# Seven products instead of eight for V and P as well: a fused decoder layer on one Trainium2 core

## The chip, the cores and the metric

The kernel runs on one core of one Trainium2 chip. The metric is the device time of one execution in microseconds (us). Three runs of the kernel before the change gave a median of 1529.9 us (1529.4 to 1530.04). All work is done by that core's engines: PE (matrix products), DVE (elementwise work on vectors), ACT (activations, copies and casts), POOL (a few small operations), and SP, whose queue issues most of the transfers.

## The reference

One decoder layer on a sequence of 256 tokens with 2048 features, in float32. What matters here is the input projection, whose columns are cut into K, Q, V, Z, P and two gates, and what becomes of them:

```python
h = rmsnorm(x, norm_mix_w[l])
proj = jnp.einsum('bsd,de->bse', h, w_in[l])
q, k, v, z, b_raw, a_raw, p_in, g_a, g_b = jnp.split(proj, splits, axis=-1)
qkv = jax.nn.silu(causal_dwconv(jnp.concatenate([q, k, v], axis=-1), conv_qkv_w[l]))
...
o = gated_delta_rule(q, k, v, g_log, beta).astype(x.dtype)
o = rmsnorm(o, gdn_norm_w[l]) * jax.nn.silu(z.reshape(bsz, seq, N_HEADS, HEAD_DIM))
pooled = causal_multiscale_pool(p_in.reshape(bsz, seq, N_POOL_GROUPS, POOL_GROUP_DIM))
y_b = jnp.einsum('bsgc,gcd->bsgd', pooled, pool_w[l]).reshape(bsz, seq, D_POOL) * pool_scale[l]
mixed = jax.nn.sigmoid(g_a) * y_a + jax.nn.sigmoid(g_b) * y_b
x = x + jnp.einsum('bsd,de->bse', mixed, w_out[l])
```

Behind it come a gated feed-forward part with 5632 inner features and a last norm.

## The kernel before, in words

**Groups, blocks, tiles.** The heads are worked on in four groups of four (`g` 0 to 3 in the code, group one to four here). A group has seven blocks of 512 columns of `w_in`, in the order K, Q, V, P, GB (gate b), Z, GA (gate a), and a small pool product. A block's weights come as eight *tiles* of 256 input features x 512 columns (512 KB each, `raw`, four buffers). ACT casts each to a rounded high part (`whi`, line 343) and DVE subtracts to get the low part (`wlo`, line 354, the *split*); both have three buffers. PE then does 12 matmuls of 128x128 by 128x512 for a plain tile: two halves of the features, two halves of the tokens, and three passes (high by high, high by low of x, low by high of x), in `gemm_a`.

**The pair of K and Q.** In groups two to four, K and Q already share a cheaper form. Two tiles of K and the same two of Q (features 0 to 511) are a 2x2 by 2x2 block product: eight block products of six matmuls each, 48, if done plainly. `pair_product` does seven products of six matmuls instead, called T1, 11, T2, 21, T3, 22 and T4. Their weights are either one of the four tiles as it is (11, 21, 22) or a difference of tiles that DVE makes (`up_sum`, line 270): T1 to T4. The four tiles are loaded into buffers of other things that are free then (`quad`, homes `KQ_HOMES`: `crow`, `mv`, `pu`, `pa`). Between the products come a copy of the first result (`own`, ACT), a copy into the second block's bank, a sum `u` (DVE, line 429), a copy of `u` into the other block's bank (ACT, line 418) before product 21 begins, and one more sum (DVE, line 431). The seven products stand in three parts: `KQ_FIRST` between the last tiles of the GA of the group before, `KQ_MIDDLE` (21, T3, 22) while GA's banks are being read out, and `KQ_THEN` (tile 2, T4, tiles 3 to 7) as the rest of K. Q then has its tiles 2 to 7.

**What goes on beside it.** `later` is a list of closures that `gemm_a` runs at a given tile (`flush`): a block's read-out is followed by its convolution (`conv_silu`: eight PE transposes, four ACT and twelve DVE instructions `cy`, a tanh, a DVE product), V's shifted copies through memory (`v_moved`, `v_conv`, tiles `mv`), and `mixed`, which turns the finished output `sz` of the group before on PE and splits it into `mhi`/`mlo`. The delta rule of a group (`gdn`) is a generator that `gemm_a` steps twice per tile; it begins with a load of `crow` and eight ACT exponentials (`dec`, line 958) and ends in the next group with `so`, `ro`, eight ACT scalings of `vt` (line 1340) and two DVE products on `sz`.

**What sets the order.** Every engine works strictly in the order of its own list. In the part in question a scheduler writes these lists from the dependencies and its own estimates when the program is built; `tc.issue_after` adds an order by hand.

## Time and profile before

| | |
|---|---|
| median of three runs | 1529.9 us |
| the profiled execution, its own time | 1531.07 us |
| its span, first to last instruction | 1529.3 us |
| PE busy | 1517.6 us, 99% of the span |
| DVE busy | 1263.2 us, 83% |
| ACT busy | 884.6 us, 58% |
| POOL busy | 73.0 us, 5% |
| moved by DMA | 313.60 MB, 205 GB/s on the mean |
| groups two to four run from about | 176 us to 700 us |

In the profile's rows a number behind a name such as L354 is the line of the kernel, a row of groups reads "line engine operation out<-in shapes xcount | busy us, mean ns of one | idle time of the engine ahead of it and what ended that", and a row of the timeline reads "start us, duration us, engine, line, ...". Matmuls overlap each other, so their recorded 390 ns or so are not what one of them costs; the distance of their starts is.

### The profile page before, as it was taken

The page shows a single profiled execution, that of the slowest core. Times are in us where ns is not written, and L with a number is a line of the kernel's source. Part 1 is how long each engine was busy: PE and PEld are TensorE (multiplying, and loading weights), DVE is VectorE, ACT ScalarE, POOL GpSimd, SP SyncE. Part 2 cuts the span into 40 slices and gives each one's busy share as a digit, 9 for nine tenths or more (in the row PEclk, how much of TensorE's full clock was granted, in tenths as well). Part 3 has the DMA queues.
Part 4 walks back from the last instruction along what each step waited for, and adds up shares of the span by engine and source line. Part 5 has one row for each costly group of instructions (what it writes and reads, how often), then busy time and mean ns, then how long its engine had stood idle before and what let it go on. Part 6 is the DMA issues. An engine that isn't in the chain of part 4 may idle for free.

```text
span 1529.3 us, 20251 instructions
## 1 busy us (share of the span) xinstructions
PE 1517.6 (99%) x7272; PEld 1252.7 (82%) x7272; DVE 1263.2 (83%) x1775; ACT 884.6 (58%) x1145; POOL 73.0 (5%) x97
## 2 busy tenths in 40 slices
PE   9999999999999999999999999999999999999998
PEld 8878888888878878788888888888888888888876
DVE  6779868888588877877567999999998886989896
ACT  7556556455556456454455677667666665555553
POOL 1000000100100001000000000000000011010200
PEclk9999999999999999999999999999999999999999
DMA  8777648784667746776588646666457468566762
GB/s 276 207 231 223 196 142 232 223 256 127 194 211 215 235 134 201 220 199 187 171 258 311 192 166 220 220 211 216 152 164 235 143 215 274 174 224 210 239 199 99
DMA packets 170097, 313.60 MB, mean 205 GB/s; under 512 B 23650, under 2 KB 27010, under 8 KB 169870
## 3 DMA queue, kind: packets, MB, share of 16 engines
q1 hardware_dynamic: 160864, 283.17, 58.7%
q0 software_dynamic: 7344, 27.27, 5.6%
q10 hardware_dynamic: 1790, 1.89, 0.4%
q8 instruction: 57, 0.93, 0.2%
q14 instruction: 42, 0.34, 0.1%
HBM read 303.33 MB, written 8.95 MB: 204 GB/s over the span
## 4 chain that ended last, share of the span: by engine, by line
PE 94%; issue 2%; DVE 2%; DMA 1%; ACT 1%; POOL 0%; POOLq 0%; DVEq 0%; ACTq 0%
PE psg L439 27%; PE psm L404 14%; PE psm L402 13%; PE psm L403 13%; PE psm L1523 7%; PE psg L1523 7%; PE psm L439 3%; PE psm L582 1%; PE psm L1591 1%; PE psg L481 1%; DVE wlo L354 1%; PE psg L969 1%; PE psg L971 0%; DMA vrow<-ev 0%; ACT whi L343 0%
## 5 line engine op out<-in xcount | busy, mean ns | idle before, releaser
L343 ACT CAST whi<-raw 128x1024 fp32r<-128x1024 f32 x408 | 427.7, 1051 | 346.2 <-PE psm L403 192.6
L354 DVE TENSOR_TENSOR wlo<-raw,whi 128x1024 fp32r<-128x1024 f32 x406 | 494.8, 1222 | 134.8 <-ACT whi L343 126.2
L343 ACT CAST whi<-quad 128x1024 fp32r<-128x1024 f32 x203 | 213.0, 1052 | 159.0 <-PE psg L439 45.4
L354 DVE TENSOR_TENSOR wlo<-quad,whi 128x1024 fp32r<-128x1024 f32 x203 | 246.8, 1223 | 39.8 <-ACT whi L343 36.6
L402 PE MATMUL psm<-whi,xhl 128*128 128x512 f32 x384 | 150.3, 392 | 0.1
L403 PE MATMUL psm<-whi,xhl 128*128 128x512 f32 x384 | 150.2, 391 | 0.0
L404 PE MATMUL psm<-wlo,xhl 128*128 128x512 f32 x384 | 139.9, 393 | 0.5 <-DVE wlo L354 0.4
L439 PE MATMUL psg<-whi,fhl 128*128 128x512 f32 x504 | 127.1, 389 | 0.0
L439 PEld LDWEIGHTS psg<-whi,fhl 128*128 128x128 f32 x504 | 94.6, 188 | 19.7
L270 DVE TENSOR_TENSOR quad<-quad,quad 128x1024 f32<-128x1024 f32 x84 | 102.5, 1220 | 0.1
L402 PEld LDWEIGHTS psm<-whi,xhl 128*128 128x128 f32 x384 | 72.1, 188 | 15.6 <-ACT whi L343 0.5
L404 PEld LDWEIGHTS psm<-wlo,xhl 128*128 128x128 f32 x384 | 71.7, 188 | 15.9 <-DVE wlo L354 1.3
L403 PEld LDWEIGHTS psm<-whi,xhl 128*128 128x128 f32 x384 | 72.1, 188 | 15.3 <-issue 0.5
L439 PE MATMUL psg<-wlo,fhl 128*128 128x512 f32 x252 | 69.8, 389 | 0.0
L439 PE MATMUL psg<-whi,ups 128*128 128x512 f32 x216 | 58.1, 391 | 0.2 <-DVE psg L1544 0.2
L439 PEld LDWEIGHTS psg<-wlo,fhl 128*128 128x128 f32 x252 | 47.3, 188 | 9.9
L1523 PE MATMUL psm<-whi,hhi 128*128 128x512 f32 (+1 forms) x140 | 54.2, 387 | 0.0
L1523 PE MATMUL psm<-whi,hlo 128*128 128x512 f32 (+1 forms) x140 | 53.7, 386 | 0.0
L402 PE MATMUL psm<-whi,mhi 128*128 128x512 f32 x128 | 50.6, 397 | 0.0
L1523 PE MATMUL psm<-wlo,hhi 128*128 128x512 f32 (+1 forms) x140 | 50.2, 386 | 0.0
L403 PE MATMUL psm<-whi,mlo 128*128 128x512 f32 x128 | 50.0, 390 | 0.0
L404 PE MATMUL psm<-wlo,mhi 128*128 128x512 f32 x128 | 48.3, 392 | 0.0
(455 smaller groups left out, 2983.3 us busy)
## 6 DMA issues: line engine op xcount, KB each, us to landing
raw<-in_w_in_dram SPq DMA_DIRECT2D x212, 512.0 KB, 4.4
raw<-in_w_up_dram SPq DMA_DIRECT2D x104, 512.0 KB, 4.9
quad<-in_w_up_dram SPq DMA_DIRECT2D x72, 512.0 KB, 5.0
raw<-in_w_down_dram SPq DMA_DIRECT2D x56, 512.0 KB, 4.7
raw<-in_w_out_dram SPq DMA_DIRECT2D x32, 512.0 KB, 4.8
quad<-in_w_down_dram POOLq DMA_DIRECT2D x32, 512.0 KB, 5.4
mv<-vrow SPq DMA_DIRECT2D x12, 512.0 KB, 4.8
quad<-in_w_in_dram SPq DMA_DIRECT2D x12, 512.0 KB, 7.4
```

The costliest lines, as they stand in the source:

```text
L270: nc.vector.tensor_tensor(out_, plus_, minus_, op=ALU.subtract)
L343: last_cast[0] = nc.scalar.copy(hi, raw).ins
L354: last_split[0] = nc.vector.tensor_tensor(lo, raw, hi.bitcast(F32), op=ALU.subtract).ins
L402: mm(ps[:, t, :], lh(k, t), hi[:, kk, :], start=(k == 0), stop=False, **seeded)
L403: mm(ps[:, t, :], ll(k, t), hi[:, kk, :], start=False, stop=False, **seeded)
L404: mm(ps[:, t, :], lh(k, t), lo[:, kk, :], start=False, stop=(k == nk - 1), **seeded)
L439: mm(ps, lhs(kk), w[n][:, kk], start=(first and n == 0 and kk == 0 and lhs is high), stop=False, skip_group_check=True)
L481: nc.tensor.transpose(pt[:, ff, t * P : (t + 1) * P], src[:, t, f * P : (f + 1) * P], ident)
L582: mm(ps_k0[:, t, :], part(k, t), w[:, kk, :], start=(k == 0 and w is hi and part is xh), stop=(k == KD - 1 and w is lo))
L969: mm(pg0, kq[:, h, 0, 0:P], kq[:, h, :, :], start=True, stop=True)
L1523: mm(ps[:, cs], lhs(kk), part_[:, kk, cs], start=(first and kk == 0 and n == 0), stop=(last and kk == 1 and n == 2), skip_group_check=shared)
L1591: nc.tensor.transpose(out_[f // 2][:, f % 2, t * P : (t + 1) * P], e[:, t, f * P : (f + 1) * P], ident)
```

## The change

V and P of groups two to four become a pair like K and Q. V's T1, 11 and T2 go between Q's last three tiles, 21, T3 and 22 stand while Q is read out, and V's own block becomes tile 2, T4 and tiles 3 to 7; P keeps tiles 2 to 7. The four tiles of this pair are loaded into `mv`, `pu`, `pa` and `dec0`, and its sum `u` into `crow`. Since V's block is now run with a flush at tile 3 (it was tile 1), as is P's, the closures behind them start two tiles later, and the generator gets no steps in the products. `mixed` of the group before is kept back in `mixing` and run behind K's convolution instead of ahead of it. The first product on `sz` behind GA is tied behind the split issued last.

```diff
+    up_w = {(pair, g): [cols(w_in[0], base + 512 * g, KD) for base in bases]
+            for pair, bases in (("kq", (C_K, C_Q)), ("vp", (C_V, C_P))) for g in range(1, 4)}
...
-            if g and base == C_K:
-                srcs += [("up", ("kq", g), step, 0) if isinstance(step, str) else tiles[step]
+            if g and base in (C_K, C_V):
+                pair = "kq" if base == C_K else "vp"
+                srcs += [("up", (pair, g), step, 0) if isinstance(step, str) else tiles[step]
                          for step in KQ_MIDDLE + KQ_THEN]
+            elif g and base == C_Q:
+                srcs += tiles[2:5]
+                srcs += [("up", ("vp", g), step, 0) if isinstance(step, str) else tiles[step] for step in KQ_FIRST]
             else:
-                srcs += tiles[2:] if g and base == C_Q else tiles
+                srcs += tiles[2:] if g and base == C_P else tiles
...
-    KQ_HOMES = ("crow", "mv", "pu", "pa")
+    KQ_HOMES = {"kq": ("crow", "mv", "pu", "pa"), "vp": ("mv", "pu", "pa", "dec0")}
...
-            bank["u"] = mp.tile([P, 512], F32, tag="dec0", name=nm("u"))
+            bank["u"] = mp.tile([P, 512], F32, tag=bank["u_home"], name=nm("u"))
...
-                ps = gemm_a(xh, xl, KD, range(2, 8), pair_bank["ps"][1], 3)
+                ps = gemm_a(xh, xl, KD, range(2, 5), pair_bank["ps"][1], 3)
+                pair_bank.update(ps=(pm(), None), u_home="crow")
+                kq_steps(KQ_FIRST, ps)
             e = evict(ps)
             convs.append(conv_silu(e, kind, g, dst))
             if g:
                 later.append(lambda conv=convs[-1]: sum(1 for _ in conv))
+                later.extend(mixing)
+                mixing.clear()
...
+        if g:
+            pair_bank["ps"] = pair_bank["ps"][0], pm()
+            kq_steps(KQ_MIDDLE, None)
...
-        e = evict(gemm_a(xh, xl, KD), rsh)
+        if g:
+            ps = pair_bank["ps"][0]
+            kq_steps(KQ_THEN, ps)
+        else:
+            ps = gemm_a(xh, xl, KD)
+        e = evict(ps, rsh)
...
-        ps = gemm_a(xh, xl, KD)
+        ps = gemm_a(xh, xl, KD, range(2, 8), pair_bank["ps"][1], 3) if g else gemm_a(xh, xl, KD)
...
-        nc.vector.scalar_tensor_tensor(sz, ta, 1.0, sz, op0=ALU.add, op1=ALU.mult)
+        with tc.issue_after(last_split[0]):
+            nc.vector.scalar_tensor_tensor(sz, ta, 1.0, sz, op0=ALU.add, op1=ALU.mult)
...
         if g < 3:
-            later.append(mixed)
+            mixing.append(mixed)
```

How the lists move is shown at three places, all in group three, around the end of Q and the start of V. In these rows `wlo<-raw` is the split of a plain tile, `wlo<-quad` that of a product's weights, `quad<-quad` a difference of tiles, `cy` a step of a convolution.

DVE before, in the first half of V: the splits of V's plain tiles, and the steps of K's convolution among them.

```order
L354 TENSOR_TENSOR wlo_3976<-raw_3972,whi_3974 128x1024
L910 SCALAR_TENSOR_TENSOR cy_3771<-psg_3761,cqw,cy_3771 128x255
L910 SCALAR_TENSOR_TENSOR cy_3771<-psg_3766,cqw,cy_3771 128x255
L910 SCALAR_TENSOR_TENSOR cy_3771<-psg_3761,cqw,cy_3771 128x254
L354 TENSOR_TENSOR wlo_4005<-raw_4001,whi_4003 128x1024
L910 SCALAR_TENSOR_TENSOR cy_3771<-psg_3766,cqw,cy_3771 128x254
```

DVE now, from V's sum `u` to the splits of V's tile 2 (`wlo_3963`) and T4 (`wlo_3974`). In this stretch the splits of T3 (`wlo_3928`) and 22 (`wlo_3951`), a difference, both small sums of the pair, `ro` of the group before and K's convolution follow one another.

```order
L435 TENSOR_TENSOR u_3924<-psm_3853,own_3864 128x512
L916 SCALAR_TENSOR_TENSOR cy_3783<-psg_3773,cqw,cy_3783 128x253
L360 TENSOR_TENSOR wlo_3928<-quad_3679,whi_3926 128x1024
L276 TENSOR_TENSOR quad_3659<-quad_3719,quad_3659 128x1024
L1162 TENSOR_TENSOR ro_3313<-ro_3313,so_3499 128x8
L916 SCALAR_TENSOR_TENSOR cy_3783<-psg_3778,cqw,cy_3783 128x253
L360 TENSOR_TENSOR wlo_3951<-quad_3699,whi_3949 128x1024
L916 SCALAR_TENSOR_TENSOR cy_3783<-psg_3773,cqw,cy_3783 128x255
L437 TENSOR_TENSOR psm_3947<-psm_3853,own_3864 128x512
L360 TENSOR_TENSOR wlo_3963<-raw_3959,whi_3961 128x1024
L360 TENSOR_TENSOR wlo_3974<-quad_3659,whi_3972 128x1024
L1165 TENSOR_SCALAR ro_3313<-ro_3313,rsq 128x4 x2
```

K's convolution has come forward into the stretch of the seven products, and more DVE work stands between one split and the next than before.

SP before, in group three: `crow` is issued without a wait of its own, among the loads of weights.

```order
L243 DMA raw_3893<-in_w_in_dram 128x2x512 [waits DMAHW6_49,DVE_49]
L243 DMA raw_3941<-in_w_in_dram 128x2x512 [waits DMAHW7_49,DVE_49]
L945 DMA crow_3961<-crd 128x1024
L862 DMA taps_3888<-in_conv_qkv_w_dram 128x512 [waits DVE_49]
L862 DMA taps_3888<-in_conv_qkv_w_dram 128x512
L243 DMA raw_3972<-in_w_in_dram 128x2x512 [waits DMAHW0_49,DVE_49]
```

SP now: the load of `crow` waits for ACT, for the copy that reads `u`, which lies in the same buffer. The next weights stand behind it.

```order
L249 DMA raw_4007<-in_w_in_dram 128x2x512 [waits DMAHW6_49,DMAHW2_49,DVE_49]
L249 DMA raw_4049<-in_w_in_dram 128x2x512 [waits DMAHW3_49,DVE_49]
L951 DMA crow_4069<-crd 128x1024 [waits Activation_49]
L249 DMA raw_4080<-in_w_in_dram 128x2x512 [waits DMAHW4_49,DVE_49]
L249 DMA raw_4109<-in_w_in_dram 128x2x512 [waits DMAHW5_49,DVE_49]
L249 DMA raw_4141<-in_w_in_dram 128x2x512 [waits DMAHW6_49,DVE_49]
```

ACT before, in group three: the scalings of `vt` come first, then four casts, and then the exponentials `dec`, of which two of eight are shown.

```order
L1340 ACTIVATE vt_2322<-psg_3379,ro_3206 128x128 x4
L1340 ACTIVATE vt_2322<-vt_2322,ro_3206 128x128 x4
L343 CAST whi_3829<-raw_3827 128x1024
L343 CAST whi_3847<-raw_3845 128x1024
L343 CAST whi_3865<-raw_3863 128x1024
L343 CAST whi_3895<-raw_3893 128x1024
L958 ACTIVATE dec_704_3959<-crow_3961,ncum 128x128
L958 ACTIVATE dec_705_3960<-crow_3961,ncum 128x128
```

ACT now, from the copy of `u` on: the casts of V's tile 2, T4 and tile 3, then the `dec` rows, of which the first two are shown.

```order
L424 COPY psm_3946<-u_3924 128x512
L913 ACTIVATE cy_3783<-psg_3773,cqw 128x256
L349 CAST whi_3961<-raw_3959 128x1024
L349 CAST whi_3972<-quad_3659 128x1024
L913 ACTIVATE cy_3783<-psg_3778,cqw 128x256
L349 CAST whi_3991<-raw_3989 128x1024
L964 ACTIVATE dec_734_4067<-crow_4069,ncum 128x128
L964 ACTIVATE dec_735_4068<-crow_4069,ncum 128x128
```

Behind the last of the eight `dec` rows come the scalings of `vt`, and only then the cast of V's tile 4 (`whi_4009`).

```order
L964 ACTIVATE dec_735_4068<-crow_4069,ncum 128x128
L1360 ACTIVATE vt_2403<-psg_3482,ro_3313 128x128 x4
L1360 ACTIVATE vt_2403<-vt_2403,ro_3313 128x128 x4
L349 CAST whi_4009<-raw_4007 128x1024
L349 CAST whi_4051<-raw_4049 128x1024
```

So `dec`, which used to stand five rows behind `vt`, now stands ahead of it, six rows behind the copy of `u` on which its load depends. Group four's lists read the same here; in group two the `vt` rows are long done.

More of the change, by code (lines that the diff above doesn't have):

```diff
@@ L85 @@
     KQ_THEN = (2, "T4", 3, 4, 5, 6, 7)
-    up_w = {("kq", g): [cols(w_in[0], base + 512 * g, KD) for base in (C_K, C_Q)] for g in range(1, 4)}
+    up_w = {(pair, g): [cols(w_in[0], base + 512 * g, KD) for base in bases]
+            for pair, bases in (("kq", (C_K, C_Q)), ("vp", (C_V, C_P))) for g in range(1, 4)}
     srcs = []
@@ L158 @@
     quads_behind = {}
-    for g in range(1, 4):
-        sums_behind[first_part(("kq", g)) - 1] = [(("kq", g), "T1", 0)]
-        for i in range(4):
-            quads_behind[first_part(("kq", g)) - 6 + i] = [(("kq", g), i)]
+    for pair in up_w:
+        if isinstance(pair, tuple):
+            sums_behind[first_part(pair) - 1] = [(pair, "T1", 0)]
+            for i in range(4):
+                quads_behind[first_part(pair) - 6 + i] = [(pair, i)]
     for n, src in enumerate(srcs):
@@ L257, in quad_load @@
         if isinstance(c, tuple):
-            home = mp.tile([P, 2, 512], F32, tag=KQ_HOMES[i], name=nm("quad"))
+            home = mp.tile([P, 2, 512], F32, tag=KQ_HOMES[c[0]][i], name=nm("quad"))
         else:
@@ L1189 @@
     pair_bank = {}
+    mixing = []
     def kq_steps(steps, ps, flush=3):
@@ L1316 @@
             ps = gemm_a(xh, xl, KD, range(5))
-            pair_bank["ps"] = pm(), None
+            pair_bank.update(ps=(pm(), None), u_home="dec0")
             kq_steps(KQ_FIRST, ps, 1)
```

## The prediction

> **What bounds the kernel now.** I read the page's totals first, then the chain that ended last, then the timeline around the longest waits.
>
> ```profile
> span 1529.3 us, 20251 instructions
> ...
> PE 1517.6 (99%) x7272; PEld 1252.7 (82%) x7272; DVE 1263.2 (83%) x1775; ACT 884.6 (58%) x1145; POOL 73.0 (5%) x97
> ...
> PEclk9999999999999999999999999999999999999999
> ```
>
> PE is the bound at a full granted clock, so time is won by fewer matmuls and lost by anything PE has to wait for. The chain of waits, merged, prices a matmul:
>
> ```profile
> 239.33 1.75 PE psg L481 x16
> ...
> 527.64 1.36 PE psm L439 x6
> ...
> 545.53 1.23 DVE sz L1323
> ...
> 546.76 1.15 DVE wlo L354
> ...
> 1315.35 2.72 PE psm L1523 x12
> ```
>
> Six matmuls take 1.36 us and twelve 2.72, 0.227 each; a transpose 0.109. Two of these rows are DVE's: there PE waited. In the timeline that is the longest wait of the groups:
>
> ```profile
> 547.95 0.50 PE L404 MATMUL psm<-wlo,xhl1a 128*128 128x512 f32 x1 [1.41 <-DVE wlo L354]
> ```
>
> It lies in the pair of K and Q ahead of group four: a product on `sz` (1.23) stood ahead of a split. So the same form of pair already costs PE some waiting where DVE has other work. How much room DVE has where the new pair goes, at the end of Q and the start of V:
>
> ```profile
> core 0: us, PE busy (x) PEld busy (x) DVE busy (x) ACT busy (x) POOL busy (x), PEclk, DMA share, GB/s
> 205.00:245.00 40.00, 40.00 (x207) 34.04 (x206) 23.15 (x31) 24.36 (x44) 2.86 (x3) 1.00 0.69 203
> 380.00:420.00 40.00, 40.00 (x206) 34.02 (x205) 21.53 (x29) 23.01 (x43) 4.42 (x3) 1.00 0.66 203
> 556.00:596.00 40.00, 40.00 (x216) 33.86 (x215) 21.80 (x28) 22.06 (x39) 4.56 (x3) 1.00 0.62 183
> ```
>
> On the mean DVE is idle for 17 to 18 of 40 us here. What counts is how far it runs ahead of PE, the *lead*: from the end of a split to PE's first use of it.
>
> ```profile
> 327.55 1.23 DVE L354 TENSOR_TENSOR wlo<-raw,whi 128x1024 fp32r<-128x1024 f32 x1 [0.29 <-ACT whi L343]
> ...
> 332.84 0.61 PE L404 MATMUL psm<-wlo,phi 128*128 128x512 f32 x2
> ...
> 554.79 3.50 DVE L354 TENSOR_TENSOR wlo<-raw,whi 128x1024 fp32r<-128x1024 f32 x3
> ```
>
> This split ends at 328.78 and its first use starts at 332.84: a lead of 4.1 us among plain tiles. Three buffers of `wlo` keep it from exceeding two plain tiles, 5.4. The third row gives DVE's pace: three splits in 3.50 us where three times 1.22 would be 3.67, so an instruction starts about 0.084 ahead of the end of the one before.
>
> **The change part by part.** *The products.* Four tiles of 12 matmuls become seven products of 6, 48 against 42, in three groups: 18 matmuls by 0.227 = **-4.1 us** on PE. With PE at 99% nothing hides that gain. *The loads* are the same four tiles per pair and move no more bytes; the homes `mv`, `pu`, `pa`, `dec0` are free by then, and the loads were issued a few tiles ahead: nothing, and if the cover goes, PE waits for a `quad` as for a tile.
>
> *DVE's and ACT's own work.* Per pair DVE gets three more splits, four differences and two sums, 3x1.22 + 4x1.22 + 0.69 + 0.70 = 9.9 us, less than the room of 17 above; ACT three more casts and three copies. What matters is where they stand. The durations:
>
> ```profile
> L354 DVE TENSOR_TENSOR wlo<-quad,whi 128x1024 fp32r<-128x1024 f32 x203 | 246.8, 1223 | 39.8 <-ACT whi L343 36.6 <-PE psm L439 1.7
> ...
> L343 ACT CAST whi<-quad 128x1024 fp32r<-128x1024 f32 x203 | 213.0, 1052 | 159.0 <-PE psg L439 45.4 <-DVE quad L270 30.7 <-DVE quad L326 21.0
> ...
> L270 DVE TENSOR_TENSOR quad<-quad,quad 128x1024 f32<-128x1024 f32 x84 | 102.5, 1220 | 0.1
> ...
> L910 DVE SCALAR_TENSOR_TENSOR cy<-psg,cqw,cy 128x255 f32<-128x255 f32 (+2 forms) x96 | 40.4, 478 | 0.7 <-ACT cy L907 0.6
> ...
> L917 DVE SCALAR_TENSOR_TENSOR kq<-th,cy 128x1024 f32<-128x1024 f32 x8 | 9.8, 1224 | 0.1
> ...
> L1154 DVE TENSOR_REDUCE so<-o 128x4 f32<-128x512 f32 x8 | 5.5, 684 | 8.3 <-ACT o L1153 8.3
> ...
> L1356 DVE TENSOR_TENSOR mlo<-psg,mhi 128x512 fp32r<-128x512 f32 x8 | 5.1, 685 | 3.8 <-ACT mhi L1355 3.8
> ...
> L1341 DVE TENSOR_TENSOR sz<-sz,vt 128x1024 f32<-128x1024 f32 x3 | 3.7, 1227 | 3.2 <-ACT vt L1340 3.2
> ...
> L431 DVE TENSOR_TENSOR psm<-psm,own 128x512 f32<-128x512 f32 x3 | 2.1, 698 | 0.1
> ...
> L429 DVE TENSOR_TENSOR u<-psm,own 128x512 f32<-128x512 f32 x3 | 2.1, 692 | 0.2 <-PE psm L439 0.2
> ...
> L1159 DVE TENSOR_SCALAR ro<-ro,rsq 128x4 f32<-128x4 f32 x8 | 1.4, 226 | 3.4 <-POOL ro L1157 3.4
> ```
>
> Group two: from the split of T1 to that of 22, DVE's list now has 33 instructions: 8 splits (9.8), 3 differences (3.7), 12 `cy` (5.7), one `so`, two products on `sz` (2.4), `kq` (1.2), `u` (0.7), two `mlo` (1.4), three small ones on `ro` (0.7): 26.3, less 30 starts 0.084 early, 23.8. Between the first uses of these two splits PE has 68 matmuls and 16 transposes, 68x0.227 + 16x0.109 = 17.2. DVE falls back by 6.6 and has a lead of 4.1 to 5.4: PE waits 1.2 to 2.5; I take **2.1**, since at such places in the pair of K and Q the lead is at its smallest.
>
> Groups three and four: from the split of 21 to that of V's tile 2 there are 16 instructions: 3 splits, a difference, 7 `cy`, `so`, `u`, the other sum, the sum on `vt` like them (0.7), one small: 3.7 + 1.2 + 3.3 + 0.7 + 0.7 + 0.7 + 0.7 + 0.2 = 11.2, paced 9.9. PE has 18 matmuls between these uses, 4.1. Against a lead of 4.1 to 5.4: 0.4 to 1.7 of waiting each, I take 1.3, **2.6** for both. Below zero none of this can go: the lists are fixed and PE cannot pass a split.
>
> *The load of `crow`.* It now waits for the copy of `u`, and the `dec` rows on ACT wait for it; behind them on ACT stand `vt` and the casts of V's tiles 4 and on, behind it on SP the next tiles, behind `vt` on DVE the product on `sz` and the split of tile 4. What a load of `crow` takes to reach `dec`, in groups three and four now:
>
> ```profile
> 407.41 0.47 SPq L945 DMA_DIRECT2D crow<-crd  x1
> ...
> 413.35 1.82 POOL L950 TENSOR_SCALAR_AFFINE_SELECT crow<-crow 128x512 f32<-128x512 f32 x2 [11.37 <-DMA crow<-crd]
> ...
> 414.62 2.45 ACT L958 ACTIVATE dec<-crow,ncum 128x128 f32<-128x128 f32 x8 [1.79 <-POOL crow L950]
> ...
> DMA to landing us min/median/max: 4.7/4.7/4.7
> ...
> 236.43 1.57 ACT L958 ACTIVATE dec<-crow,ncum 128x128 f32<-128x128 f32 x5 [2.10 <-POOL crow L950]
> ```
>
> From 407.41 to 414.62 is 7.2 us; 4.7 to landing and POOL's 0.7 alone would be 5.4 or a little over. ACT waited 2 us for it even where nothing held it back. The scalings cost
>
> ```profile
> L1340 ACT ACTIVATE vt<-psg,ro x12: 359/368/377, 228.8 to 589.3; 128x128 f32<-128x128 f32 x12
> ...
> L1340 ACT ACTIVATE vt<-vt,ro x12: 403/412/416, 229.8 to 590.4; 128x128 f32<-128x128 f32 x12
> ```
>
> about 0.3 each in sequence (the eight `dec` of 0.39 took 2.45). Counted from the end of the copy of `u`, ACT ends the cast of tile 4 at 5.8 to 7.2 + 2.4 + 2.5 + 1.05 = 11.8 to 13.2. PE, from the same moment, has 22, tile 2, T4 and tile 3 to do: 1.36 + 2.72 + 1.36 + 2.72 = 8.2, and waits 1.3 for DVE: 9.5. So it waits another 2.3 to 3.7; I take 2.5 in each of the groups three and four, **5.0**. If the copy comes earlier against PE than I think, it is 0. In group two `vt` is done before, the cast of tile 4 ends at 9.3 to 10.7 against PE's 8.2 + 2.1 = 10.3: nothing.
>
> [...]
>
> *The product on `sz`* behind the split: the wait of 1.41 shown above goes, and by the same running sum the smallest lead of that pair is then 0.4, so the next thing late is that pair's tile 2: **-1.4** (0 to -1.5). *K's convolution ahead of `mixed`* adds no instruction; it is in the sums above, since it brings the `cy` among the products. *`v_conv`* starts later, and DVE waits in it for memory already:
>
> ```profile
> 448.05 1.23 DVE L887 TENSOR_TENSOR mv<-mv,taps 128x1024 f32<-128x1024 f32 x1 [4.02 <-DMA mv<-vrow]
> ```
>
> With the lead smaller on arrival I add **1.0** (0 to 3). The generator loses 8 of its steps per group; in group four it has to be at its last part by GA's tile 6, and has steps to spare.
>
> Sum: -4.1 + 2.1 + 2.6 + 5.0 - 1.4 + 1.0 = **+5.2 us**. The profiled execution took 1531.07 (span 1529.3 and 1.8 around it), so it would take 1536.3; against the median of 1529.9 that is **1535.1 us**.
>
> **The rivals.** A measurement of this kernel can tell about 0.2%, 3.1 us, from no change.
>
> *Faster: DVE's room hides it all.* The windows speak for it (10 us of new work into 17 of room), the running sums against. If PE waits nowhere anew: -4.1 - 1.4 = 1524.4 us. It decides itself in group two: if the lead ahead of T1 is over 6.6, there is no wait.
>
> *No change: `crow` comes in time.* If `u` is copied 2.5 us or more ahead of product 22, ACT is not late and the term of 5.0 goes: 1530.1. For it: PE might itself be held up ahead of 22 by the splits, and time that PE stands still there counts for the load.
>
> *Slower still: the clock falls.* If PE stands still so long that its clock is halved for a while, one plain tile takes 2.72 us more in each of two groups: 1535.1 + 5.4 = 1540.5. Against it: the longest wait shown is 1.41 us, and the granted clock stays at 9 throughout. [...]
>
> **How the numbers follow.** My forecast with `crow` late gets 0.55, `crow` in time 0.27, everything hidden 0.10, the clock 0.08. The forecast's own range is 1531 to 1539: the lower ends (1.2, 0.8, 4.6, -1.5, 0) give 1531, the upper ones (2.5, 3.4, 7.4, 0, 3) 1542, and not all fall together. The range for 8 in 10 leaves the hidden case out below and most of the clock's above: 1527 to 1541. Faster by over 0.2%: 0.10. Within 0.2% (to 1533.0): `crow` in time, and a little of my forecast's lower end, 0.33. Slower: the rest, 0.57.
>
> **What would show it.** Right: 18 matmuls of 512 fewer; in groups three and four a wait of PE at the split of V's tile 2, with DVE full, and a longer one at tile 4, with ACT idle until `crow` and `dec` and `vt` ahead of the cast; in group two a wait at 22 or tile 2; no wait behind GA's `sz`. Wrong: leads over 1 us through all of V, which would mean that the sums leave out room; or PE waiting for a transfer of `quad` or `raw` instead, which I have at nothing.

## The result, and the profile after

The changed kernel took 1542.78 us in the median of its runs (1542.14 to 1544.14) against 1529.97 for the kernel before, a ratio of 1.0085 with a 95% interval of 1.0072 to 1.0097: 12.8 us slower. The forecast was 1535.1, with a range of 1527 to 1541. The direction was right; the size was not, and the time lies above the range.

The page's totals and the shares of the chain that ended last, after:

```profile
span 1541.1 us, 20281 instructions
...
PE 1521.1 (99%) x7254; PEld 1248.5 (81%) x7254; DVE 1292.9 (84%) x1802; ACT 897.6 (58%) x1163; POOL 74.2 (5%) x97
...
PE 93%; DMA 2%; ACT 1%; DVE 1%; issue 1%; POOL 0%; SPq 0%; POOLq 0%; ACTq 0%; DVEq 0%
```

PE has 18 instructions fewer (7254 against 7272), as the products promise. The span is 11.8 us longer all the same, and the share of transfers in the chain is 2%, where it was 1%. To find the places I took, for every matmul, the distance from its start to the next start, less the median distance of its shape (0.227 us for 128x512). Over all of PE the excess is 24.7 us before and 40.6 after: 15.9 more, less 4.1 for the 18 matmuls, is the 11.8. By place, counting only excesses above 0.06 us:

| place | before | after | difference | the prediction's term |
|---|---|---|---|---|
| 18 matmuls fewer | | | -4.1 | -4.1 |
| group two: end of Q, 22, V's tile 2 | 0.3 | 2.6 | +2.3 | +2.1 |
| groups three and four: end of Q, 22, V's tile 2 | 0.2 each | 1.8 each | +3.2 | +2.6 |
| groups three and four: V's tile 4 | 0 | 2.2 each | +4.4 | +5.0 |
| group two: V's tile 4 | 0 | 1.5 | +1.5 | 0 |
| pair of K and Q ahead of group three, T1 to T4 | 1.5 | 4.1 | +2.7 | 0 |
| pair of K and Q ahead of group four, T1 to T4 | 2.4 | 1.4 | -0.9 | -1.4 |
| the rest of K in groups three and four | 1.0 | 3.8 | +2.8 | 0 |
| `v_conv` in group three | 0.7 | 0 | -0.7 | +1.0 |
| elsewhere, and all below 0.06 | | | +0.6 | 0 |

**V's tile 4.** The chain of waits in group three, after (start, duration, what):

```profile
426.00 0.49 ACT psm L424
...
426.51 3.66 DMA crow<-crd
...
430.33 1.91 POOL crow L956
...
432.27 1.34 ACT dec L964 x5
...
434.72 2.19 ACT vt L1360 x8
```

That is the chain the prediction wrote down, link for link: the copy of `u` ends at 426.49, `crow` is loaded, POOL masks it, the eight `dec` run, then the eight `vt`, and only then ACT can cast tile 4. The timeline of the same stretch has what PE sees of it:

```profile
432.27 2.45 ACT L964 ACTIVATE dec<-crow,ncum 128x128 f32<-128x128 f32 x8 [2.18 <-POOL crow L956]
434.63 1.11 ACT L1360 ACTIVATE vt<-psg,ro 128x128 f32<-128x128 f32 x4
435.63 1.28 ACT L1360 ACTIVATE vt<-vt,ro 128x128 f32<-128x128 f32 x4
436.79 2.00 ACT L349 CAST whi<-raw 128x1024 fp32r<-128x1024 f32 x2
...
437.89 0.50 PE L408 MATMUL psm<-whi,xhl2a 128*128 128x512 f32 x1 [0.99 <-ACT whi L349]
```

**The pair ahead of group three.** The longest wait of the changed kernel is one that the prediction did not have. Timeline, after; `tbd` and `TT` are the trip through memory by which the generator turns its small triangular blocks `T`:

```profile
364.24 2.53 SPq L1046 DMA_DIRECT2D tbd<-tb  x4
...
368.27 3.21 SPq L1049 DMA_DIRECT2D TT<-tbd  x4
...
371.68 0.43 DVE L1061 STREAM_TRANSPOSE T<-TT 32x256 f32<-32x256 f32 x1 [3.20 <-DMA TT<-tbd]
...
372.17 0.31 PE L1085 MATMUL psg<-T,ga 32*32 32x32 f32 x4 [2.00 <-DVE T L1061]
```

PE stands for 2.0 us because the generator's matmul on `T` is next in its list and the trip is not over. Before, the same trip began at 343.56 us, some 21 us earlier:

```profile
343.56 2.53 SPq L1040 DMA_DIRECT2D tbd<-tb  x4
...
350.62 0.43 DVE L1055 STREAM_TRANSPOSE T<-TT 32x256 f32<-32x256 f32 x1 [1.97 <-DMA TT<-tbd]
...
352.65 0.20 PEld L1079 LDWEIGHTS psg<-T,ga 32*32 32x32 f32 x4 [0.35 <-PE psm L439]
```

And the wait has a second part. The granted clock in the two stretches of 3.41 us from 369.15 on (columns as in the windows above; the clock is the figure ahead of the DMA share):

```profile
369.15:372.56 3.41, 1.41 (x11) 0.86 (x9) 0.88 (x2) 1.85 (x2) 0.00 (x0) 1.00 0.27 43
372.56:375.97 3.41, 3.41 (x10) 2.53 (x11) 3.25 (x6) 0.00 (x0) 0.00 (x0) 0.50 0.68 168
```

PE is idle for 2.0 of 3.41 us, and its clock stands at 0.50 for the next 3.41, which costs about 1.7 us more.

The rest of K, behind this pair and the next, loses about 1.4 us more per group though PE has no long wait there. The generator's small matmuls on `T`, 32x32 each, stood among the large ones in five pieces before, all five within the pair ahead of group three and three within that ahead of group four. Now they come in eight pieces, six of them behind the pair, and around each piece the starts of PE's matmuls lose about 0.3 us.

### The profile page after: what moved, and what is told of

Read it like the earlier page. It is cut to its first block, busy times and chain, and to the rows that moved or that the text cites. A ratio compares the mean times of both kernels' runs of the same rounds, so it can differ in the third digit from the quotient of the medians.

```text
span 1541.1 us, 20281 instructions
## 1 busy us (share of the span) xinstructions
PE 1521.1 (99%) x7254; PEld 1248.5 (81%) x7254; DVE 1292.9 (84%) x1802; ACT 897.6 (58%) x1163; POOL 74.2 (5%) x97
## 4 chain that ended last, share of the span: by engine, by line
PE 93%; DMA 2%; ACT 1%; DVE 1%; issue 1%; POOL 0%; SPq 0%; POOLq 0%; ACTq 0%; DVEq 0%
PE psg L445 28%; PE psm L410 13%; PE psm L408 13%; PE psm L409 13%; PE psm L1543 7%; PE psg L1543 7%; PE psm L445 3%; PE psm L588 1%; PE psm L1611 1%; PE psg L975 1%; DMA crow<-crd 1%; PE psg L487 1%; DVE wlo L360 1%; PE psg L977 0%; ACT dec L964 0%
## 5 line engine op out<-in xcount | busy, mean ns | idle before, releaser
L349 ACT CAST whi<-raw 128x1024 fp32r<-128x1024 f32 x396 | 415.5, 1052 | 325.4 <-PE psm L409 181.7
L360 DVE TENSOR_TENSOR wlo<-raw,whi 128x1024 fp32r<-128x1024 f32 x394 | 479.6, 1220 | 123.3 <-ACT whi L349 114.5
L349 ACT CAST whi<-quad 128x1024 fp32r<-128x1024 f32 x224 | 235.3, 1053 | 174.8 <-PE psg L445 44.0
L360 DVE TENSOR_TENSOR wlo<-quad,whi 128x1024 fp32r<-128x1024 f32 x224 | 272.0, 1220 | 49.6 <-ACT whi L349 46.0
L409 PE MATMUL psm<-whi,xhl 128*128 128x512 f32 x336 | 131.4, 391 | 0.0
L408 PE MATMUL psm<-whi,xhl 128*128 128x512 f32 x336 | 131.3, 391 | 0.0
L410 PE MATMUL psm<-wlo,xhl 128*128 128x512 f32 x336 | 123.3, 393 | 0.0
L276 DVE TENSOR_TENSOR quad<-quad,quad 128x1024 f32<-128x1024 f32 x96 | 116.9, 1218 | 0.1
L408 PEld LDWEIGHTS psm<-whi,xhl 128*128 128x128 f32 x336 | 63.1, 188 | 13.2
L409 PEld LDWEIGHTS psm<-whi,xhl 128*128 128x128 f32 x336 | 63.1, 188 | 13.1
L410 PEld LDWEIGHTS psm<-wlo,xhl 128*128 128x128 f32 x336 | 62.6, 188 | 13.2 <-DVE wlo L360 0.4
```

Of the source, the lines that this page charges most:

```text
L276: nc.vector.tensor_tensor(out_, plus_, minus_, op=ALU.subtract)
L349: last_cast[0] = nc.scalar.copy(hi, raw).ins
L360: last_split[0] = nc.vector.tensor_tensor(lo, raw, hi.bitcast(F32), op=ALU.subtract).ins
L408: mm(ps[:, t, :], lh(k, t), hi[:, kk, :], start=(k == 0), stop=False, **seeded)
L409: mm(ps[:, t, :], ll(k, t), hi[:, kk, :], start=False, stop=False, **seeded)
L410: mm(ps[:, t, :], lh(k, t), lo[:, kk, :], start=False, stop=(k == nk - 1), **seeded)
```

## The experiments

All times are medians, with the ratio to the kernel before and its 95% interval. Before's own median was 1529.8 to 1530.0 in these runs. "After" is the changed kernel, 1542.8.

### The generator's steps

```diff
-LATE = (26, 24, 22, 18)
+LATE = (26, 16, 14, 10)
```

> The changed kernel with the generator's idle steps cut by eight in groups two to four, the number that the products took from it; nothing else. Theory 1 (the wait of 2.2 us at 369.8 us, on the transfer of T through memory, comes from the eight missing steps): that wait goes and with it the 3.4 us at half clock behind it, so the time falls by about 4 us to 1539. Rival (the transfer is slow or late for another reason, such as its place on the queue): a wait of 1 us or more on T stays, and the time with it. What is behind 370 us in the generator then comes earlier by four tiles, which may also move the time at the pair ahead of group four by 1 us either way.

Measured: 1536.71 us, 1.0041 (1.0029 to 1.0054): 6.1 us less than after. The trip to `T` begins at 347.9 us again, and neither the wait nor the halved clock is there (the mean granted clock of the profiled run is 0.998, as in the kernel before, where it was 0.997 after):

```profile
347.94 2.54 SPq L1046 DMA_DIRECT2D tbd<-tb  x4
...
353.69 1.42 DVE L1061 STREAM_TRANSPOSE T<-TT 32x256 f32<-32x256 f32 x3 [1.05 <-DMA TT<-tbd]
...
356.65 0.31 PE L1085 MATMUL psg<-T,ga 32*32 32x32 f32 x4
```

The gain in the pair ahead of group three and the K behind it is 3.9 us, and in the K of group four 1.6. At V's tile 4 the waits fell too, from 1.5, 2.2 and 2.2 to 0.7, 0.7 and 1.5 us; in groups three and four the eight `vt` no longer stand ahead of that cast (in group three they end 11 us before the copy of `u`). On the other side the waits at the end of Q and at 22 and tile 2 rose from 1.8 to 2.6 us in groups three and four: with the generator on time, DVE's list in the products there became that of group two, with `kq`, two `sz` and two `mlo` in it. So the eight missing steps cost more than the wait on `T`, and hid 0.8 us of DVE's shortage in each of two groups.

### dec out of the way of the casts

```diff
                 for t, dec in ((0, dec0), (1, dec1)):
+                  with tc.issue_after(last_cast[0]):
                     nc.scalar.activation(dec[:, h, :], crow[:, h, t, :], AF.Exp,
```

> The changed kernel with each dec tied behind the cast that was issued last; u stays in crow. ACT's order is the same up to the cast of V's tile 3; then the eight vt and three casts (V's tiles 4 to 6) come, and the eight dec behind them. Theory 1 (ACT stands for crow with the casts of V's tile 4 and on queued behind dec): the waits at tile 4 (1.5, 2.2 and 2.2 us) go or shrink to vt's share, under 0.7 us each; 4 to 6 us less than 1542.8, near 1538. Rival (the raw load of tile 4 itself is late, behind crow on SP's queue): the waits stay within 0.5 us.

Measured: 1538.87 us, 1.0055 (1.0042 to 1.0067): 3.9 us less than after. ACT's rows in group three now:

```profile
423.57 0.60 ACT L424 COPY psm<-u 128x512 f32<-128x512 f32 x1
...
429.99 1.15 ACT L1361 ACTIVATE vt<-psg,ro 128x128 f32<-128x128 f32 x4 [2.22 <-DVE ro L1166]
431.00 1.29 ACT L1361 ACTIVATE vt<-vt,ro 128x128 f32<-128x128 f32 x4
432.17 2.01 ACT L349 CAST whi<-raw 128x1024 fp32r<-128x1024 f32 x2
...
436.74 2.45 ACT L965 ACTIVATE dec<-crow,ncum 128x128 f32<-128x128 f32 x8
```

From the end of the copy of `u` (424.17) to the end of tile 4's cast, the first of the two in one row, are about 9.0 us, where it was 11.3, and at V's tile 4 PE waits 0, 0.7 and 0.7 us in the three groups where it was 1.5, 2.2 and 2.2. `dec` itself costs nothing where it now stands. The tiles' own loads, behind `crow` on the queue, were not what was late: the rival falls.

### Both, and whether they add up

> The changed kernel with eight idle steps fewer and dec tied behind the cast issued last; K's convolution stays where the change put it, so DVE's list in the products is the same in groups two to four. If the two causes add up, the waits at tile 4 that the steps alone left (0, 0.5 and 1.3 us) go: 1535 (1536.7 less 1.8), and what is left above 1525.8 (1529.9 less the 4.1 of the matmuls) is DVE's: 0.39 + 0.97 + 0.57 us and some tenths in each group. Rival (the tie moves other rows): 1537 or more, with a wait that is not there without the tie.

Measured: 1532.07 us, 1.0014 (1.0005 to 1.0023): 10.7 us less than after, and 3 better than I expected. At tile 4 nothing is left in any group (under 0.06 us each). What is left is the same three waits in groups two, three and four, at the end of Q, at 22 and at tile 2, 2.6 us in each group. (The one at the end of Q, 0.5 of it, is for ACT's read-out of Q, and ACT itself had waited 0.4 us for a split just before.) Of DVE in group three there:

```profile
419.21 1.22 DVE L923 SCALAR_TENSOR_TENSOR kq<-th,cy 128x1024 f32<-128x1024 f32 x1
...
420.35 0.68 DVE L435 TENSOR_TENSOR u<-psm,own 128x512 f32<-128x512 f32 x1
420.95 1.22 DVE L360 TENSOR_TENSOR wlo<-quad,whi 128x1024 fp32r<-128x1024 f32 x1
422.08 1.22 DVE L276 TENSOR_TENSOR quad<-quad,quad 128x1024 f32<-128x1024 f32 x1
423.22 1.28 DVE L1377 TENSOR_TENSOR mlo<-psg,mhi 128x512 fp32r<-128x512 f32 x2
424.42 1.21 DVE L360 TENSOR_TENSOR wlo<-quad,whi 128x1024 fp32r<-128x1024 f32 x1
425.55 1.21 DVE L360 TENSOR_TENSOR wlo<-raw,whi 128x1024 fp32r<-128x1024 f32 x1
425.68 0.30 PEld L445 LDWEIGHTS psm<-wlo,xs 128*128 128x128 f32 x2 [1.23 <-DVE wlo L360]
```

Each instruction starts 0.08 to 0.09 us before the one ahead of it ends, and PE takes the low weights of 22 0.05 us after they are there (425.63). At these places that is 7.1 us more than in the kernel before. Less the 4.1 of the matmuls, 1.3 gained in the pair ahead of group four and the K behind it, and 0.7 at `v_conv`, it is +1.0, which is what the span grew by (1530.3 against 1529.3); the medians differ by 2.1.

### K's convolution later in the program

```diff
-                ps = gemm_a(xh, xl, KD, range(2, 5), pair_bank["ps"][1], 3)
+                ps = gemm_a(xh, xl, KD, range(2, 5), pair_bank["ps"][1], 9)
```

> The changed kernel with K's convolution run from V's tile 3 on, behind the seven products, as Q's is; nothing else. Theory 1 (DVE is short in the products): the twelve cy leave the stretch, 5.7 us of DVE, and the waits at 22 and at V's tile 2 (1.6 us in group two, 1.0 in each of groups three and four) go: 3.6 us less. Rival A (ACT and the load of crow set the end of the stretch): PE gains at tile 2 what it loses at tile 4, 0 change. Rival B (two convolutions and mixed in one place): DVE falls behind in V's later tiles instead, and the time rises by 1 to 4 us.

Measured: 1540.57 us, 1.0068 (1.0054 to 1.0081), 2.2 us less. At the end of Q, 22 and tile 2 the waits fell from 2.6 to 2.0 us in group two and from 1.8 to 0.8 in group three; in group four they stayed at 1.8. Those at V's tile 4 went in all three groups, 5.9 us, which I had not expected. Against that the pair ahead of group four lost 3.0 us, and at 718 to 728 us, with the generator still late, PE waited for `T` and then ran at half clock, 4.8 us more than after (the mean granted clock of the profiled run is 0.994, after 0.997). My reading of the edit was too simple: by the order of the list, nine `cy` still stand among the products of group two. The scheduler ranks the convolution behind the splits now, but fills gaps with it.

> The changed kernel with eight idle steps fewer, and K's convolution run from V's tile 3 on. With the steps cut alone, each of the groups two to four has waits of 0.39 (the turning of Q), 0.97 (22's low weights) and 0.57 us (V's tile 2), behind a DVE that does not stop from u to tile 2. Theory 1 (DVE is short in the products, by K's convolution): they shrink to half or less, 3 to 5 us less than 1536.7, 1531.7 to 1533.7. Rival (the two small sums, the mlo and the seven splits alone keep DVE behind): within 1 us of 1536.7. Rival B (the convolutions pile up from tile 3): waits of 1 us or more appear in V's tiles 4 to 7 or in P.

Measured with the steps cut as well: 1530.20 us, 1.0001 (0.9992 to 1.0009), 6.5 us less than with the steps alone. That is more than theory 1 said, but only a part of it lies where theory 1 put it. At the end of Q, 22 and tile 2 the waits fell from 1.9 us in each group to 1.3, 1.1 and 1.8 (excesses above 0.25). Counting every distance, these places gave 2.0 us, and V's tile 4, where PE had waited for ACT's cast and then for the split and nothing is left, gave 3.0. With that the products just pay for what they bring. With four steps fewer (26, 20, 18, 14) and with twelve (26, 12, 10, 6):

> As the run with eight idle steps fewer and K's convolution issued later (1530.2), but four steps fewer. If the wait on T is a matter of the steps, it comes back here in part: with four steps (two plain tiles, 5.4 us) less in hand than with eight, T may be in time still (1530 to 1531) or late by up to 1 us. Rival (the exact number decides the order everywhere): 1532 or more by waits elsewhere.

> The same with twelve idle steps fewer. If eight is enough, more earliness gains nothing: 1530.2 within 1 us. Rival: the generator's rows come into GB and Z, where DVE has room, and the pair ahead of the next group is freer: 1528 to 1529.

Measured: 1531.72 (1.0012; 1.0003 to 1.0021) and 1530.75 (1.0007; 0.9998 to 1.0015). Four were nearly enough, more than eight gains nothing.

### All of K's convolution held back

The two ties below (the second run has only the first of them) go on top of the kernel with eight steps fewer and K's convolution later.

```diff
-                nc.vector.scalar_tensor_tensor(y[:, f, s:], gs[:, : S - s], w(j), y[:, f, s:],
...
+                with tc.issue_after(last_split[0]) if g and kind else ExitStack():
+                    nc.vector.scalar_tensor_tensor(y[:, f, s:], gs[:, : S - s], w(j), y[:, f, s:],
...
-                nc.vector.tensor_tensor(ml[:, fs, :], pt, mh[:, fs, :].bitcast(F32), op=ALU.subtract)
+                with tc.issue_after(last_split[0]) if g < 3 else ExitStack():
+                    nc.vector.tensor_tensor(ml[:, fs, :], pt, mh[:, fs, :].bitcast(F32), op=ALU.subtract)
```

> The changed kernel with eight idle steps fewer, K's convolution issued from V's tile 3 on, and each cy of it and each mlo of mixed tied behind the split issued last, so that no cy and no mlo stands among the products on DVE (by the lists: 7 splits, 2 differences, u and in group two two sz products from T1's split to tile 2's). Theory 1 (DVE's shortage there is K's convolution and mixed): the waits at 22 and tile 2 go in all three groups, and the 4.1 us of the fewer matmuls show: 1526 to 1528. Rival A (the seven splits, differences and sums alone are too much): waits of 1 us or more per group stay there, about 1530. Rival B (the work comes back in one lump in V's tiles 4 to 7): waits of 1 us or more there, 1531 or more.

> The same without the tie on mlo: only the cy of K's convolution are tied. Theory 1 with the convolution as the main part: the same time as with both ties within 1 us. Rival (the two mlo, 1.3 us, matter too where they fall among the products, which is group two): 0.5 to 1.5 us more than with both.

Measured: 1546.39 us, 1.0110 (1.0094 to 1.0125), and 1548.97, 1.0114 (1.0095 to 1.0133). The intervals overlap, so the two cannot be told apart. By the time this is rival B. In group two no excess above 0.25 us is left at the end of Q or in V, so the convolution and `mixed` are indeed what DVE was short by there. In groups three and four 1.1 and 1.6 us stay at the products (the same count) without a `cy` or an `mlo` among them; there the late rows of the generator, `so`, the sum on `vt` and the products on `sz`, stand between the splits. And the work has to be done, and what needs its result comes later, behind V and not in V's tiles 4 to 7: in group three a wait of 2.2 us where P ends, with DVE standing 2.4 us for V's shifted copy, 5 us of waits in the pair of K and Q ahead of group four, 2.7 us on `T` in group four, and a halved clock behind each of the three (the mean granted clock of the first run's profile is 0.994, after 0.997). In all that is 16 us more than with the convolution free to fill gaps.

### u in another buffer

If the copy of `u` no longer holds `crow`, the load can come early. This looked like the same test as the tie of `dec`. It was not.

```diff
-                pair_bank.update(ps=(pm(), None), u_home="crow")
+                pair_bank.update(ps=(pm(), None), u_home="th")
```

> The changed kernel with V's sum u in the buffer th, which lies idle there, in place of crow; nothing else. Theory 1 (the load of crow behind the copy of u holds up ACT): the waits of PE at the first use of V's tile 4, 1.1 to 1.2 us with 0.2 to 0.8 behind them, in the groups two to four (1.5, 2.2 and 2.2 us) go, so the time falls by 4 to 6 us from 1542.8 to about 1537.5. Rival (the eight dec and the eight vt scalings are simply too much for ACT in these products, wherever crow comes): they now stand ahead of the casts of 22 and tile 2, the wait moves there, and the time stays within 2 us of 1542.8.

> Both edits together: u in th, and eight idle steps fewer in groups two to four. If the two waits are independent, as I think, the time falls by the sum of the two single edits, 8 to 10 us, to about 1533; the rest of the loss is then DVE's in the products (about 3.5 us). Rival (they share a cause, DVE's or ACT's load in the products): the sum is less than the larger single gain plus 1 us.

Measured: 1568.24 (1.0247; 1.0233 to 1.0261) and 1556.07 (1.0169; 1.0155 to 1.0183). My choice of buffer was wrong: `th` is written by the tanh of K's convolution in that very stretch, so the copy of `u` came behind it. The same with `w1`, which is free:

```diff
-                pair_bank.update(ps=(pm(), None), u_home="crow")
+                pair_bank.update(ps=(pm(), None), u_home="w1")
```

> The changed kernel with V's sum u in the buffer w1 in place of crow. In the run with u in th that buffer was not idle: the tanh of K's convolution writes it, and the copy of u came behind it. w1 (the generator's) is read for the last time before so. Theory 1 (the load of crow behind the copy of u holds up ACT ahead of V's tile 4): the waits there (1.5, 2.2 and 2.2 us) go, 4 to 6 us less than 1542.8. Rival (eight dec and eight vt scalings are too much for ACT here wherever crow comes): with crow early four dec stand ahead of the casts of 22 and tile 2, the waits at tile 4 turn into waits there, and the time stays within 2 us.

> The changed kernel with u in w1 and eight idle steps fewer in groups two to four. With the steps cut alone (1536.7 us) the vt scalings are out of the products, and the waits at V's tile 4 are 0, 0.6 and 1.4 us. Theory 1 (what is left there is crow's): they go too, 2 us less, 1534.7. Rival (with vt out of the way crow has time enough, and what is left there is ACT's own queue): no change, 1536.7.

> All three: u in w1, eight idle steps fewer, K's convolution behind the products. If crow, the steps and DVE's shortage are three separate causes, nearly all of the new waits go and the 4.1 us of the fewer matmuls show: 1527 to 1530, at or below the kernel before. If what is left is the products' own splits, 1531 to 1534.

Measured: 1545.40 (1.0097; 1.0083 to 1.0111), 1553.76 (1.0154; 1.0140 to 1.0168) and 1543.67 (1.0088; 1.0074 to 1.0101): slower by 2.6, 17.1 and 13.5 us than the same kernels with `u` in `crow`. Group three of the second:

```profile
427.11 1.15 SPq L951 DMA_DIRECT2D crow<-crd  x1
...
436.72 1.22 POOL L956 TENSOR_SCALAR_AFFINE_SELECT crow<-crow 128x512 f32<-128x512 f32 x2 [21.27 <-DMA crow<-crd]
437.39 1.28 ACT L964 ACTIVATE dec<-crow,ncum 128x128 f32<-128x128 f32 x4 [4.71 <-POOL crow L956]
438.58 1.03 ACT L349 CAST whi<-raw 128x1024 fp32r<-128x1024 f32 x1
...
439.66 0.79 PE L408 MATMUL psm<-whi,xhl1b 128*128 128x512 f32 x1 [4.13 <-ACT whi L349]
```

The load now takes 9.6 us from issue to POOL, where it took 3.8 after the copy of `u`, and the scheduler, which thought it would be early, put `dec` ahead of the cast of tile 3. ACT stands for it 4.7 us and PE 4.1. In the first of the three runs, with `u` in `w1` alone, group two goes the same way: 10.8 us from issue to POOL, ACT stands 5.9 us, and the places from the end of Q to V's tile 4 lose 10.3 us, half a clock included (0.996 on the mean of the profiled run, after 0.997), where they lost 4.1 after. But groups three and four of that run do what theory 1 said. Group three:

```profile
424.01 0.46 SPq L951 DMA_DIRECT2D crow<-crd  x1
...
430.32 1.28 ACT L964 ACTIVATE dec<-crow,ncum 128x128 f32<-128x128 f32 x4 [0.63 <-POOL crow L956]
...
434.89 0.59 ACT L424 COPY psm<-u 128x512 f32<-128x512 f32 x1
```

`crow` is issued 11 us ahead of the copy of `u` and is there after 5.6; ACT waits 0.6 us for it, no wait is left at V's tile 4, and the same places lose 2.0 and 1.7 us in groups three and four where they lost 4.0 each. So the mechanism holds (ACT stands at `dec` for `crow`, with casts behind it). The remedy helps where the load comes before `dec` is reached, and costs more than it gains where the scheduler has put `dec` ahead of a cast and the load takes 10 us. Why the same 512 KB take so differently long is taken up at the end.

### Three more

`mixed` back to where it was before the change, with the steps cut and K's convolution later:

```diff
         if g < 3:
-            mixing.append(mixed)
+            later.append(mixed)
```

> The changed kernel with eight idle steps fewer, K's convolution behind the products, and mixed run at K's tile 3 as in the kernel before. With the first two edits the time was 1530.2 and waits of 1.3, 1.1 and 1.8 us were left at 22 and V's tile 2. Theory 1 (what is left is DVE's, and the two mlo are 1.3 us of it): waits of 0 to 0.6 per group, 1527 to 1529. Rival (with mixed early, vt's scalings come into the products and ACT is late for 22 or tile 2): 1531 or more.

Measured: 1543.42 (1.0088; 1.0074 to 1.0102). In group two no excess above 0.25 us is left, which is what theory 1 says. In groups three and four 2.0 us stay at the products, and ACT again stands for `crow` with casts behind `dec`, 5.8 us in group three; PE loses 3.8 us ahead of V's tile 5 there and runs at half clock behind it (its starts at 439.44 and 439.87 are 0.43 us apart, where the median is 0.227):

```profile
424.63 0.33 SPq L951 DMA_DIRECT2D crow<-crd  x1
...
434.75 1.23 POOL L956 TENSOR_SCALAR_AFFINE_SELECT crow<-crow 128x512 f32<-128x512 f32 x2 [23.84 <-DMA crow<-crd]
435.42 2.44 ACT L964 ACTIVATE dec<-crow,ncum 128x128 f32<-128x128 f32 x8 [5.80 <-POOL crow L956]
```

The tie of `dec` on the kernel with the steps cut and K's convolution later:

> The changed kernel with eight idle steps fewer, K's convolution behind the products, and dec tied behind the last cast. No waits at tile 4 were left without the tie (1530.2), so by theory 1 it gains nothing, 1530.2 within 1.5 us. Rival (dec was still in the way of the casts of V's tiles 2 and 3): 1527 to 1529. Since the tie also lets the order of the other rows on DVE change (some cy and two products on sz stand among the products now), a loss of 1 to 4 us would speak for DVE as the short one there.

Measured: 1532.30 (1.0018; 1.0009 to 1.0027). The tie gains nothing where there was no wait at tile 4, as theory 1 says; it lets other rows move, two waits of 1.0 and 0.9 us on `T` come at 711 us, and the time is 2.1 us longer than without it.

The one line of the change that stands alone, in the kernel before:

```diff
-        nc.vector.scalar_tensor_tensor(sz, ta, 1.0, sz, op0=ALU.add, op1=ALU.mult)
+        with tc.issue_after(last_split[0]):
+            nc.vector.scalar_tensor_tensor(sz, ta, 1.0, sz, op0=ALU.add, op1=ALU.mult)
```

> The kernel before with one line of the change alone: the first product on sz tied behind the split issued last. By the prediction the wait of 1.41 us ahead of group four goes: 1528.5, within the noise of 0.2%, so it is to be read in the profile. Rival (the product falls ahead of the next split instead): another wait of about 1 us in the same pair, no change.

Measured: 1529.09 us, 0.9994 (0.9986 to 1.0003). In its profile no excess above 0.25 us is left in any of the three pairs of K and Q: the wait of 1.41 is gone. A gain of 0.7 us, with an interval that holds both 1.4 and nothing.

No version beat both kernels beyond doubt. The best with the new pair is level with the kernel before.

## Why the prediction was right or wrong

- *The products, -4.1:* right; 18 instructions fewer.
- *DVE's shortage in the products, +2.1 and +2.6:* right, 2.3 and 3.2, at the places named (22 and tile 2 in group two, tile 2 in the others); 0.7 of the 2.3, and 0.3 in each of the others, stand at the end of Q, which it did not name. With the two other causes taken away, it is all that is left, 2.6 us in each group. What the running sum could not see is that groups three and four had the smaller shortage only because the generator was late.
- *`crow` in groups three and four, +5.0:* right in mechanism, and 4.4 in size. From the end of the copy of `u` to `dec` took 5.8 us, the lower end of what was added up: the load took 3.7 us and not 4.7, but POOL's part ahead of `dec` 1.9 and not 0.7. The cast of tile 4 ended 11.3 us after the copy, not 11.8 to 13.2, since the eight `vt` took 2.2 us and not 2.5 and a row starts 0.09 to 0.12 us before the end of the one ahead. PE came to tile 4 after 10.3 us, not 9.5. The cause is shown by the tie of `dec`. The three loads took 3.5 to 6.7 us from issue to POOL.
- *`crow` in group two, 0:* wrong by 1.5. PE came 10.3 us after the copy, as forecast, but the cast ended at 11.4, not at 9.3 to 10.7: the load took 6.6 us there. The chain of waits, and the timeline:

```profile
245.25 0.50 ACT psm L424
...
245.76 6.57 DMA crow<-crd
```

```profile
253.71 2.45 ACT L964 ACTIVATE dec<-crow,ncum 128x128 f32<-128x128 f32 x8 [4.19 <-POOL crow L956]
256.06 1.98 ACT L349 CAST whi<-raw 128x1024 fp32r<-128x1024 f32 x2
...
257.14 0.50 PE L408 MATMUL psm<-whi,xhl2a 128*128 128x512 f32 x1 [0.92 <-ACT whi L349]
```

- *The generator's steps, at nothing:* this is the step that failed. The prediction saw that the generator "loses 8 of its steps per group", looked at group four alone, found that it "has steps to spare" there, and stopped. It had steps to spare nowhere else: its trip through memory began 21 us later, PE waited 2.0 us for `T` ahead of group three and lost another 1.7 to the clock, its small matmuls cost 2.8 us in K, and the `vt` scalings came into the products. In the pair ahead of group three and in K that is 5.5 of the 11.8 us, where the prediction had nothing. Cutting the steps gave 6.1 us back.
- *The wait behind `sz`, -1.4:* the wait went, as said, and the pair ahead of group four gained 0.9. A wait on `T` of 0.4 us and one of 0.6 at tile 2's split, the next thing late that the prediction named, took a part of its place.
- *`v_conv`, +1.0:* wrong, -0.7. In the changed kernel PE does not wait at it.
- *The rivals.* "The clock falls" came true in part, at a place that I did not name: PE was idle for 2.0 us within one stretch of 3.41 ahead of group three, and the granted clock was 0.50 in the next. That a plain tile takes 2.72 us more in each of two groups, the term of 5.4, no run shows; in its place the changed kernel lost about 1.7 us to the clock, once. Its 1540.5 was nearer to the result than my own sum, for reasons that were not those.

The terms that I had and those that were missing come to 11.2 us of the 11.8 in the profile. The other 0.6 is scattered in tenths; its cause stays open.

## What to carry to other kernels

When a change takes slots away from work that is run in slots beside a loop, follow that work to its own next deadline in every round, not only in the last one: what it sends through memory leaves that much later (here by 21 us). In a list that an engine works through in order, look for the instruction that waits for a load and ask what stands behind it; moving that instruction behind the urgent work was worth 3.9 us. Making its load earlier took the wait away in two groups of three and made a longer one in the third, so that the whole was slower: a scheduler that is told that something is early may put its user first, and then the load must really be early.

## What the runs showed of the hardware that I had not expected

The granted clock fell behind some waits of PE and not behind others of the same length. After, PE was idle for 2.0 us of the 3.41 from 369.15 on, and the clock was 0.50 in the next 3.41 (rows above). In the run with both ties, of all of K's convolution and of `mixed`, PE waited 2.08 us where P ends in group three, and behind that its starts at 464.27 and 464.70 are 0.43 us apart, as those at 373.74 and 374.17 are after, in the stretch at 0.50; the median is 0.227. In the run with `dec` tied it waited 2.10 us for the same `T` as after:

```profile
366.63:370.04 3.41, 1.83 (x9) 1.17 (x7) 0.14 (x1) 2.67 (x3) 0.00 (x0) 1.00 0.21 34
370.04:373.45 3.41, 2.23 (x13) 1.58 (x14) 3.25 (x6) 0.00 (x0) 0.00 (x0) 1.00 0.58 165
```

1.58 and 1.18 us are idle in these two stretches, and the clock stays at 1.00. So the length of the wait alone does not tell whether the clock falls; what else decides is not shown.

The load of `crow`, 512 KB, took between 3.5 and 10.8 us from issue to POOL in these traces. In the four rows below, the slower loads go with a higher share of busy time of the core's 16 DMA engines meanwhile (the figure ahead of the last: 0.34 and 0.64 for loads of 3.81 and 5.64 us, 0.98 for those of 6.72 and 10.75). First the load after the change in groups three and two, then the run with `u` in `w1`, groups three and two:

```profile
426.51:430.32 3.81, 3.49 (x13) 1.83 (x11) 3.81 (x7) 3.57 (x5) 1.64 (x1) 1.00 0.34 138
245.76:252.48 6.72, 5.52 (x27) 3.98 (x26) 6.72 (x10) 2.83 (x4) 0.00 (x1) 1.00 0.98 258
```

```profile
424.01:429.65 5.64, 5.64 (x35) 4.95 (x34) 3.83 (x8) 3.41 (x5) 0.00 (x1) 1.00 0.64 186
242.26:253.01 10.75, 7.01 (x32) 4.59 (x30) 9.69 (x12) 5.17 (x8) 0.00 (x0) 1.00 0.98 216
```

In the quick one nothing but `crow` itself was moved, 0.5 MB; in the two slow ones 1.7 and 2.3 MB, with `taps` and tiles of weights issued up to 6 us ahead of it. In group two the run with `w1` issues the load 3.5 us earlier than after the change and has it half a microsecond later. No run changes this alone, so the cause is read from the traces and not shown.
